# Moving three of the six modulation vectors from beside the inverse to beside the chunk scan

## The chip, the cores and the metric

The kernel runs on one core of a Trainium2 chip, as one launch. The metric is the time on the device, in microseconds (us). A core has five engines that run their own instruction streams and meet at semaphores: TensorE (PE, with its weight loads shown apart as PEld), VectorE (DVE), ScalarE (ACT), GpSimd (POOL) and SyncE (SP, which here only starts transfers). The profile is one execution, recorded by the hardware.

## The reference, cut to what matters

Two transformer blocks are computed for one sequence of 512 tokens and 1024 features. The change lies in the first one:

```python
c_act = jax.nn.silu(c)
mod = c_act @ w_ada[l] + b_ada[l]                  # [1, 6 * 1024]
shift1, scale1, gate1, shift2, scale2, gate2 = jnp.split(mod, 6, axis=-1)
h = modulate(rms_norm(x, norm_mix[l]), shift1, scale1)
proj = h @ w_in[l]
...
gdn_out = gated_deltanet(...)                      # (I + M)^-1 per chunk, then a scan over 8 chunks
swa_out = sliding_window_attention(...)
mixed = jnp.concatenate([gdn_out, swa_out], axis=-1) @ w_out[l]
x = x + gate1[:, None, :] * mixed
h2 = modulate(rms_norm(x, norm_ffn[l]), shift2, scale2)
x = x + gate2[:, None, :] * hierarchical_moe(h2, ...)
```

So `shift1`, `scale1` are needed at the start, `gate1` in the output projection, `shift2` and `scale2` for the router after it, and `gate2` at the end of the experts. The weights `w_ada` are 24 MB in float32, 4 MB for each vector. The second block (two feed-forward layers, an attention and a recurrence) follows and is not touched.

## The kernel before, in words

Activations lie transposed, 128 features on the partitions and 512 tokens along them. Float32 products are made exact by splitting each operand into a head and a rest (`wsplit`, L252, on ACT and DVE) and multiplying three times (`mm3`, L262: lines 268, 269 and 270).

**The vectors.** `ada` (L375) is a generator. Its items are pairs (g, h): half h (512 columns) of vector g. An item takes five steps. Each of the first four (L381 to L391) loads two k-tiles of the weights, 512 KB, into one of three `wraw` buffers (L384, issued by SP), and multiplies them as the moving operand by a column of silu(c): four products of 256 columns, in four strips of 32 columns of the array, which the trace shows as eight L388 instructions. They add up in a PSUM tile of the `sm` set, which has three buffers. The fifth step (L392 to L399) adds the bias (L393), copies the sums out of PSUM on ACT (L395), folds them with four small products (L397) and copies the result into `mod` (L398).

**The order of the work.** Generators are woven by hand. `weave(main, (gen, rate))` (L193) advances a filler by `rate` steps after each step of the main generator. The tile framework's planner then orders the instructions by this program order and by its own model of when they are ready; an engine runs its list strictly in that order.

The stages around the change:

- *Inverse stage* (L842 to L848). Main: `kprep` (16 steps), `mpreps` (12) and `inverse` (56), 84 steps in all. Fillers: `dense` (the projections of q, of the window attention, of v and z, 0.6 steps), `ada` for gate1, shift2, scale2 and gate2 (eight items, 40 steps, rate 0.6) and `side` (the inner products of the chunks and the window attention, 1.2). At 0.6 the 40 steps of `ada` end after 67 of the 84 main steps.
- *Scan stage* (L965 to L967). Main: `uw` (12 steps; L855) and `scan` over the eight chunks (24 steps; L887). Filler at 0.8: `swasplit` (4 steps), `bias_tables` (2), `yd_zero` (1, which zeroes 4 MB in DRAM by a POOL transfer) and `wout_swa` (L957, 16 steps: the half of the output projection whose input is the window attention). These 23 steps end after 29 of the 36 main steps.
- *Second half of the output projection* (L989 to L997): eight rounds of twelve matmuls with the router's logits between them. Before it, L971 reads scale2 and L977 shift2.

After that come the experts (`moe`), which read gate2 last. `wraw` is shared by all of this: the loads of the projections' weights (L249) and those of `ada` (L384) take the same three buffers, in the order in which SP has them.

Of the kernel before, what the change touches and what calls it, by code (L numbers as in the profile page):

```python
# [18 lines left out]
P = 128  # L19
# [11 lines left out]
# --------------------------------------------------------------------------  # L31
# host side: layout of the inputs and constants that depend on shapes alone
# --------------------------------------------------------------------------
def _mt(w, cols=None):
    """[K, M] -> [M/128, 128 (k), K/128, 128 (m)]"""
    if cols is not None:
        w = w[:, cols]
    k, m = w.shape
    return np.ascontiguousarray(w.reshape(k // P, P, m // P, P).transpose(2, 1, 0, 3))


def _cols(v):
    """[n*128] -> [128, n]"""
    return np.ascontiguousarray(np.asarray(v).reshape(-1, P).T)


def layout(a):
    o = {}
# [38 lines left out]
    # block 2  # L87
# [23 lines left out]
    def lru(n):  # L111
        w = a[n][0].reshape(4, 2, P, 2, P)  # head, k tile, k, m tile, m
        return w.transpose(2, 0, 3, 1, 4).reshape(P, 8 * 2 * P)
# [15 lines left out]
def constants():  # L129
# [8 lines left out]
    # [t, c]: t <= c / t > c inside a chunk  # L138
# [31 lines left out]
    # relative position: one-hot bucket rows and a mask row, over u  # L170
# [14 lines left out]
# --------------------------------------------------------------------------  # L185
# device side
# --------------------------------------------------------------------------
# [5 lines left out]
def weave(main, *fill):  # L193
    """the steps of main, and after each one `rate` steps of every filler (gen, rate)"""
    due = [0.0] * len(fill)
    for _ in main:
        for i, (gen, rate) in enumerate(fill):
            due[i] += rate
            while due[i] >= 1.0:
                due[i] -= 1.0  # L200
                next(gen, None)


class Net:
# [16 lines left out]
    def bt(self, shape, dt=F32):  # L221
        """a 2 KB per partition tile out of the shared set"""
# [23 lines left out]
    # ---- weights: raw f32 -> 12-bit head (f32r) + exact rest (f32r)  # L246
# [15 lines left out]
    def mm3(self, ps, wh, wl, xh, xl, kts, start=True, stop=True):  # L262
        """ps += W^T x over the k-tiles; wh/wl [128, nk*128]; xh/xl lists of [128, N]"""
# [8 lines left out]
    def mm3y(self, ps, wh, wl, xh, xl, kts, start=True, stop=True, n=3):  # L272
        """mm3 in steps of n k-tiles"""
# [10 lines left out]
    # ---- rsqrt of a small tile (x > 0), Newton on the vector engine  # L284
# [11 lines left out]
    # ---- softplus of a small tile  # L296
# [20 lines left out]
    # ---- 1/rms over the features of a T-layout activation, broadcast to all partitions  # L317
    def sumsq(self, acc, k, src):
        """acc += src^2"""
# [7 lines left out]
    def sumsq2(self, acc, k, src, hs):  # L327
        """acc[:, hs] += src[:, hs]^2, without the tensor engine or the vector engine"""
# [7 lines left out]
    def rstd_half(self, hf, *accs):  # L336
        """[P, 2]: 1/rms of the tokens of a half; the sums over the features on the tensor engine"""
# [36 lines left out]
    # ---------------------------------------------------------------- block 1  # L374
    def ada(self, items, raws=None):  # L375
        """mod[:, g] = w_ada^T silu(c) + b_ada by halves: the k-tiles as moving operand in four column tiles"""
# [49 lines left out]
    def block1(self):  # L426
# [39 lines left out]
        # statistics of x  # L466
# [5 lines left out]
        # scale1, shift1 by halves; k-tiles 0..3 of the projections of k follow the first halves  # L472
# [50 lines left out]
        # conv + silu (twice the value)  # L523
# [14 lines left out]
        def stats2(src, pst, base):  # L538
            """pst[:, i, base:base+2] = per token sums of squares over the two 64-halves"""
# [10 lines left out]
        # ---- gates  # L550
        def gates():
            # four k-tiles beside each other in the columns of the array
# [23 lines left out]
        def decays():  # L576
# [4 lines left out]
            # sum over a chunk, per head on the partitions of its half  # L581
# [12 lines left out]
        # ---- k: token major, normalised, and back  # L594
# [32 lines left out]
        # ---- decay and -M, its transpose  # L627
# [30 lines left out]
        # ---- q, v  # L658
# [11 lines left out]
        # ---- attention inside chunks, transposed, over k  # L670
# [19 lines left out]
        # ---- projections of the window attention  # L690
# [46 lines left out]
        # ---- sliding window attention  # L737
# [59 lines left out]
        # ---- z  # L797
# [7 lines left out]
        # ---- (I + M)^-1 by doubling of the diagonal blocks  # L805
# [37 lines left out]
        ada = mark("ada", self.ada([(g, h) for g in (2, 3, 4, 5) for h in range(2)]))  # L843
# [8 lines left out]
        # ---- scaled v and k, token major, behind the inverse  # L852
        vb, kd, nw = MT, kt, [None] * 4

        def uw():  # L855
# [11 lines left out]
            for i in range(4):  # L867
# [3 lines left out]
                # -w^T [d (head parity), pair, chunk parity * 64]  # L871
# [11 lines left out]
        # ---- scan over the chunks; o = s o', s = rq / 8: s rsqrt(s^2 mean(o'^2) + eps)  # L883
# [62 lines left out]
        # results of the experts: rows for the first and the second expert of a token  # L946
# [7 lines left out]
        # ---- output projection: the rows of the window attention, then those of the delta rule  # L954
# [10 lines left out]
        fill = chain(swasplit(), self.bias_tables(), yd_zero(), wout_swa())  # L965
        weave(chain(uw(), scan()), (fill, 0.8))
        drain(fill)  # L967

        # router: logits = (x * rstd * gain + shift) W = rstd * (x (gain W)) + shift W
# [34 lines left out]
    # ------------------------------------------------- block 1: mixture of experts  # L1004
    def moe(self):
# [5 lines left out]
        # the pairs of one group at a distance: its experts tend to be in demand together  # L1011
        order = [4 * g + i for i in range(4) for g in range(4)]
        NP = NE // 2
        # the results of the last pairs go to x by the tensor engine, the others by DRAM
        NL = 2

        def load(n, part=(0, 1)):
            """weights of pair n: gate | up in two halves per expert, down"""
# [15 lines left out]
        # slots beyond the last token keep finite values  # L1034
# [4 lines left out]
        # ---- normalized tokens, token-major, and a copy in DRAM  # L1039
# [13 lines left out]
        # ---- routing  # L1053
# [3 lines left out]
        def first_max(l, n, tag):  # L1057
            """the maximum, one-hot of its first place"""
# [24 lines left out]
        # [tok, tile, expert]  # L1083
# [10 lines left out]
        # tokens of the same expert before a token: in its tile, and in the tiles before (last: all)  # L1094
# [7 lines left out]
        # place of a token at its experts, from 1  # L1102
# [9 lines left out]
        # weights of the two experts  # L1112
# [20 lines left out]
        # pair: token, weights at its two experts, rows of the results  # L1133
# [6 lines left out]
        # tiles of the passes beyond the first  # L1140
        q1, q2, q3, q4 = (self.t(self.tp, [P, S], "cy" if q < 2 else "th") for q in range(4))
        # (no reuse of an index that a transfer may still read)
# [3 lines left out]
        def oindex(p, r):  # L1146
            """place of a slot's row in yd, or its token (the last pairs); its token"""
# [14 lines left out]
        def select(p, r):  # L1162
            """slots 64r..64r+63 of the two experts of the p-th pair: one-hot by token; token and weight of a slot"""
# [19 lines left out]
        def gather(p, r):  # L1183
            """their tokens, one on a partition"""
# [8 lines left out]
        def feed(xTs, hf, pt):  # L1193
            """gain and shift of the tokens, features on the partitions"""
# [19 lines left out]
        def pick(oh):  # L1214
            """the same by the tensor engine, without the way through DRAM"""
# [11 lines left out]
        def piece(p, c, o, r):  # L1227
            """512 columns of the weights of an expert of pair p"""
# [30 lines left out]
        def expert2(p, hT, idx, wv, r=0):  # L1259
            """weighted results, to DRAM; of the last pairs: in two parts, with the one-hot of the tokens by slot"""  # L1260
# [23 lines left out]
        def combine(ys, hs):  # L1284
            """x += gate * the results of the slots, at their tokens"""
# [13 lines left out]
        def ahead(p):  # L1299
            """the passes of pair p beyond the first: tokens fetched early"""  # L1300
# [11 lines left out]
        def more(p):  # L1312
            """the second and third pass of pair p"""
# [9 lines left out]
        def rest(p, r=3):  # L1323
            """the passes beyond, with weights loaded again"""
# [564 lines left out]
```

## Time and profile before

| | us |
|---|---|
| time, median of 3 runs (2240.81 to 2242.68) | 2241.49 |
| span of the profiled execution, first to last instruction | 2238.9 |
| what lies around the span, against the median | 2.6 |
| PE busy in matmuls | 2095.0 (94%) |
| PEld busy in weight loads | 1567.7 (70%) |
| DVE busy | 1078.0 (48%) |
| ACT busy | 718.2 (32%) |
| POOL busy | 202.9 (9%) |

Shares are of the span. A stretch A:B counts us from the span's start. "Idle before, releaser" in a row is the time in which the engine stood before that group and what ended it. A matmul's time in the trace includes its way through the array, so consecutive ones overlap; what one costs is read from the starts. Each float32 matmul with a float32 weight stands as two instructions.

### The profile page before, as it was taken

The page shows a single profiled execution, that of the slowest core. Times are in us where ns is not written, and L with a number is a line of the kernel's source. Part 1 is how long each engine was busy: PE and PEld are TensorE (multiplying, and loading weights), DVE is VectorE, ACT ScalarE, POOL GpSimd, SP SyncE. Part 2 cuts the span into 40 slices and gives each one's busy share as a digit, 9 for nine tenths or more (in the row PEclk, how much of TensorE's full clock was granted, in tenths as well). Part 3 has the DMA queues.
Part 4 walks back from the last instruction along what each step waited for, and adds up shares of the span by engine and source line. Part 5 has one row for each costly group of instructions (what it writes and reads, how often), then busy time and mean ns, then how long its engine had stood idle before and what let it go on. Part 6 is the DMA issues. An engine that isn't in the chain of part 4 may idle for free.

```text
span 2238.9 us, 32214 instructions
## 1 busy us (share of the span) xinstructions
PE 2095.0 (94%) x12908; PEld 1567.7 (70%) x12908; DVE 1078.0 (48%) x2071; ACT 718.2 (32%) x1197; POOL 202.9 (9%) x223
## 2 busy tenths in 40 slices
PE   5999999788888978999999899999999999999996
PEld 3677677553333427888888787878878888888886
DVE  4663655542221227553354864746564447542444
ACT  3432442122222224322222443525452243222221
POOL 3020002011111122000001300000000031000002
PEclk9999999788999988999999999999999999999998
DMA  7343315075968962323332232323222322233321
GB/s 262 112 133 105 105 48 160 29 284 215 399 238 329 382 249 95 99 90 91 102 92 82 88 83 76 113 67 113 62 99 90 108 76 81 93 89 95 98 90 38
DMA packets 93877, 294.53 MB, mean 132 GB/s; under 512 B 15746, under 2 KB 27010, under 8 KB 81404
## 3 DMA queue, kind: packets, MB, share of 16 engines
q1 hardware_dynamic: 86364, 278.03, 36.4%
q0 software_dynamic: 7328, 14.01, 1.9%
q8 instruction: 119, 1.95, 0.4%
q14 instruction: 66, 0.54, 0.1%
HBM read 286.12 MB, written 20.23 MB: 137 GB/s over the span
## 4 chain that ended last, share of the span: by engine, by line
PE 57%; DVE 3%; POOL 1%; ACT 1%; issue 1%; POOLq 0%; ACTq 0%; DVEq 0%
PE mm L269 18%; PE mm L270 18%; PE mm L268 18%; PE sm L1605 1%; DVE xl L1507 1%; PE mm L1633 1%; POOL x L1459 1%; POOL ss L334 1%; DVE cy L1458 0%; PE mm L1630 0%; ACT wh L255 0%; PE sm L1620 0%; PE sm L1757 0%; PE mm L1289 0%; PE sm L1603 0%
## 5 line engine op out<-in xcount | busy, mean ns | idle before, releaser
L268 PE MATMUL mm<-xh,wh 128*128 128x512 f32 (+1 forms) x1584 | 621.4, 395 | 8.4 <-ACT xh L1506 4.1
L269 PE MATMUL mm<-xl,wh 128*128 128x512 f32 (+1 forms) x1584 | 612.4, 387 | 4.0 <-DVE xl L1507 4.0
L270 PE MATMUL mm<-xh,wl 128*128 128x512 f32 (+1 forms) x1584 | 609.7, 386 | 0.1
L255 ACT ACTIVATE wh<-wraw 128x1024 fp32r<-128x1024 f32 (+3 forms) x282 | 274.1, 974 | 771.8 <-PE mm L269 681.4
L256 DVE TENSOR_TENSOR wl<-wraw,wh 128x1024 fp32r<-128x1024 f32 (+3 forms) x282 | 315.0, 1118 | 196.6 <-ACT wh L255 191.3
L268 PEld LDWEIGHTS mm<-xh,wh 128*128 128x128 f32 x1584 | 301.4, 191 | 81.5 <-issue 8.3
L269 PEld LDWEIGHTS mm<-xl,wh 128*128 128x128 f32 x1584 | 303.1, 191 | 66.1 <-DVE xl L1507 5.7
L270 PEld LDWEIGHTS mm<-xh,wl 128*128 128x128 f32 x1584 | 302.6, 191 | 62.9 <-issue 1.2
L334 POOL TENSOR_TENSOR ss<-ss,sq 128x256 f32<-128x256 f32 (+1 forms) x69 | 66.9, 970 | 951.6 <-ACT sq L333 935.5
L268 PE MATMUL mm<-hh,wh 128*128 128x512 f32 (+1 forms) x416 | 149.8, 360 | 0.0
L270 PE MATMUL mm<-hh,wl 128*128 128x512 f32 (+1 forms) x416 | 149.6, 360 | 0.0
L269 PE MATMUL mm<-hl,wh 128*128 128x512 f32 (+1 forms) x416 | 149.4, 359 | 0.0
L1241 PE MATMUL mm<-wmoe,xgT 128*64 128x512 f32 x512 | 128.5, 659 | 8.1 <-issue 8.1
L1241 PEld LDWEIGHTS mm<-wmoe,xgT 128*64 128x64 f32 x512 | 42.8, 152 | 83.8 <-issue 76.4
L268 PEld LDWEIGHTS mm<-hh,wh 128*128 128x128 f32 x416 | 78.1, 188 | 13.3
L269 PEld LDWEIGHTS mm<-hl,wh 128*128 128x128 f32 x416 | 78.1, 188 | 13.3
L270 PEld LDWEIGHTS mm<-hh,wl 128*128 128x128 f32 x416 | 78.0, 188 | 13.2
L1567 DVE TENSOR_TENSOR sq<-mm,rsb 128x512 f32<-128x512 f32 x44 | 30.4, 691 | 110.7 <-PE mm L270 110.7
L1562 DVE TENSOR_TENSOR cy<-mm,rsb 128x512 f32<-128x512 f32 x44 | 30.4, 691 | 91.6 <-PE mm L270 89.6
L1247 DVE SCALAR_TENSOR_TENSOR mth<-mth,mm 128x256 f32<-128x256 f32 x16 | 6.7, 420 | 114.3 <-ACT mth L1246 114.3
L1275 PE MATMUL mm<-wmoe,hT 128*64 128x512 f32 x256 | 57.9, 592 | 0.0
L1198 ACT ACTIVATE xgT<-mm,mod,gs 128x128 f32<-128x128 f32 x64 | 27.9, 462 | 77.4 <-DVE xgT L1200 69.8
(495 smaller groups left out, 2613.7 us busy)
## 6 DMA issues: line engine op xcount, KB each, us to landing
wmoe<-in_wmoe SPq DMA_DIRECT2D x96, 1024.0 KB
wraw<-in_win SPq DMA_DIRECT2D x90, 512.0 KB
wraw<-in_wgu SPq DMA_DIRECT2D x88, 512.0 KB
wraw<-in_wada SPq DMA_DIRECT2D x32, 512.0 KB
wraw<-in_wd SPq DMA_DIRECT2D x32, 448.0 KB
big<-in_wada SPq DMA_DIRECT2D x16, 512.0 KB
wraw<-in_wd SPq DMA_DIRECT2D x16, 512.0 KB
wraw<-in_wout SPq DMA_DIRECT2D x16, 256.0 KB
```

The lines of the kernel that those rows point to most:

```text
L255: self.nc.scalar.activation(h[:, :n], raw[:, :n], AF.Copy)
L256: self.nc.vector.tensor_sub(l[:, :n], raw[:, :n], h[:, :n])
L268: mm(ps, w1, xh[k], start=start and i == 0, stop=False)
L269: mm(ps, w1, xl[k], start=False, stop=False)
L270: mm(ps, w2, xh[k], start=False, stop=stop and i == nk - 1)
L334: self.nc.gpsimd.tensor_add(acc[:, hs], acc[:, hs], sq[:, hs])
L1198: s.activation(xTs[hf][:, k, :], pt[:, k, :], AF.Identity, scale=self.gs2[:, kk:kk + 1], bias=mod[:, 3, kk:kk + 1])
L1241: mm(pg_[cs, :], xT[k // 4][:, k % 4, cs], piece(p, c, k // 4 * 2048 + k % 4 * S, r), start=k == 0, stop=k == KT - 1)
L1275: mm(py[cs, :], hT[:, k, cs], piece(p, c, 4096 + k * 1024 + n * S, r), start=k == 0, stop=k == 1)
L1459: (self.nc.gpsimd if k % 2 else self.nc.vector).tensor_add(self.x[k][:, hs], self.x[k][:, hs], t[:, hs])
L1562: v.tensor_mul(t1, pp[0], rb)
L1567: v.tensor_mul(t2, pp[1], rb)
```

## The change

The list of `ada` beside the inverse is cut from eight items to two (gate1 alone). The other six, shift2, scale2 and gate2, go beside the scan: a new helper, `alternate`, takes one step of the old filler and one of `ada` in turn until both are at an end, and the filler's rate goes from 0.8 to 1.5. (Comments are taken out elsewhere in the file, which shifts line numbers.)

```diff
+def alternate(*gens):
+    gens = list(gens)
+    while gens:
+        for gen in list(gens):
+            try:
+                next(gen)
+            except StopIteration:
+                gens.remove(gen)
+                continue
+            yield
...
-        ada = mark("ada", self.ada([(g, h) for g in (2, 3, 4, 5) for h in range(2)]))
+        ada = self.ada([(2, h) for h in range(2)])
         side = chain(after(["q", "m"], inner()), after(["swaproj"], swa()))
         weave(chain(kprep(), mark("m", mpreps()), inverse()), (dense, 0.6), (ada, 0.6), (side, 1.2))
...
-        fill = chain(swasplit(), self.bias_tables(), yd_zero(), wout_swa())
-        weave(chain(uw(), scan()), (fill, 0.8))
+        ada = self.ada([(g, h) for g in (3, 4, 5) for h in range(2)])
+        fill = alternate(chain(swasplit(), self.bias_tables(), yd_zero(), wout_swa()), ada)
+        weave(chain(uw(), scan()), (fill, 1.5))
         drain(fill)
```

No buffer, tile or shape changes. Nothing waits for the name `ada` that `mark` set.

## Rows read from the trace of the kernel before

**Rows 1.** The page, TensorE's granted clock in 40 slices of 56 us.

```profile
PEclk9999999788999988999999999999999999999998
```

**Rows 2.** Stretches: us, busy us (instructions) by engine, granted clock, DMA share, GB/s.

```profile
125.00:285.00 160.00, 159.95 (x2336) 119.43 (x2334) 87.81 (x180) 52.42 (x113) 10.27 (x8) 1.00 0.36 113
285.00:349.00 64.00, 62.15 (x746) 46.10 (x746) 31.92 (x73) 25.27 (x64) 1.89 (x2) 1.00 0.29 102
349.00:369.00 20.00, 17.23 (x311) 12.85 (x309) 9.20 (x15) 9.03 (x21) 6.22 (x11) 1.00 0.42 110
369.00:404.00 35.00, 34.21 (x386) 24.95 (x386) 26.69 (x73) 6.05 (x10) 6.18 (x10) 1.00 0.34 84
404.00:433.50 29.50, 17.66 (x213) 15.03 (x211) 19.10 (x55) 3.78 (x6) 1.23 (x2) 0.68 0.06 19
433.50:466.00 32.50, 32.50 (x126) 20.56 (x125) 10.29 (x16) 8.21 (x13) 0.62 (x1) 0.92 0.61 240
...
421.00:433.50 12.50, 6.84 (x64) 6.68 (x62) 7.30 (x22) 1.26 (x2) 0.00 (x0) 0.50 0.00 0
```

**Rows 3.** Groups of instructions by line, 125 to 286 us, those of `ada`.

```profile
L388 PE MATMUL sm<-wraw,ca 128*32 128x256 f32 x184 | 16.5, 391 | 0.0
L397 PE MATMUL sm<-c_sel,sq 128*128 128x1 f32 x48 | 6.2, 250 | 0.0
...
L395 ACT COPY sq<-sm 128x512 f32<-128x512 f32 x6 | 3.5, 587 | 13.2 <-PE sm L388 13.2
...
L393 PE MATMUL sm<-c_bada,c_ident 128*128 128x4 f32 x12 | 1.7, 210 | 0.0
```

**Rows 4.** PE's timeline around one step of `ada`: start, us, what.

```profile
257.46 0.39 PE L269 MATMUL mm<-xl,wh 128*128 128x512 f32 x1
257.68 0.40 PE L270 MATMUL mm<-xh,wl 128*128 128x512 f32 x1
258.01 0.64 PE L388 MATMUL sm<-wraw,ca 128*32 128x256 f32 x8
258.58 1.15 PE L1408 MATMUL mm<-big,big 64*64 64x64 f32 x32
```

**Rows 5.** PE's timeline around the closing step of an item.

```profile
284.62 0.28 PE L393 MATMUL sm<-c_bada,c_ident 128*128 128x4 f32 x2
284.75 1.03 PE L397 MATMUL sm<-c_sel,sq 128*128 128x1 f32 x8
285.71 0.50 PE L1408 MATMUL mm<-big,big 64*64 64x64 f32 x9
```

**Rows 6.** PE's waits from 285 to 349 us: us in total, times, longest.

```profile
PE mm L1408 <- ACT xx L812: 1.2, 1, 1.2
PE sm L793 <- ACT ptS L791: 0.4, 1, 0.4
```

**Rows 7.** PE's timeline at the end of the scan.

```profile
429.44 1.08 PE L939 MATMUL sm<-c_ident,eo 128*128 128x128 f32 x4 [5.66 <-DVE eo L934]
...
434.17 0.63 PE L269 MATMUL mm<-xl,wh 128*128 128x512 f32 x1
434.59 0.63 PE L270 MATMUL mm<-xh,wl 128*128 128x512 f32 x1
...
438.43 0.39 PE L270 MATMUL mm<-xh,wl 128*128 128x512 f32 x1
```

**Rows 8.** SP's timeline: the issue of one load of `ada`.

```profile
100.09 0.37 SPq L384 DMA_DIRECT2D wraw<-in_wada  x1
```

**Rows 9.** Stretches of 1 us after that issue; the last number is GB/s.

```profile
101.00:102.00 1.00, 1.00 (x7) 0.35 (x5) 1.00 (x3) 0.24 (x1) 0.96 (x1) 0.50 0.79 121
102.00:103.00 1.00, 1.00 (x10) 0.19 (x9) 0.90 (x5) 0.39 (x1) 0.00 (x0) 0.50 0.90 350
103.00:104.00 1.00, 1.00 (x7) 0.85 (x4) 0.90 (x5) 0.63 (x1) 0.02 (x1) 0.55 0.22 70
```

**Rows 10.** SP's waits from 300 to 450 us: us in total, times, longest.

```profile
SPq L249 <- DVE wl L256: 104.3, 12, 26.2
```

## The prediction

> **What bounds the kernel now.** I read the page first, for the share of each engine and the clock in 40 slices. TensorE is the busiest engine, and its clock stands below full speed longest in the slices from 392 to 560 us [rows 1]; the first of them holds most of the scan. Next I read busy times by stretch, with borders where the stages of the code begin and end [rows 2]. Three things are to be seen there.
>
> In the part of the inverse stage that holds `ada`, 125 to 285 us, matmuls cover 159.95 of 160 us. After the last `ada` step, 285 to 349 us, they still cover 62.15 of 64. So TensorE sets the pace there, with or without `ada`, and work that is taken out shortens the stage.
>
> In the scan stage, 349 to 433.5 us, PE is idle for 2.77 us in the first stretch (`uw`), 0.79 in the second (the scan while the old filler lasts) and 11.84 in the third (the filler has run out after 29 of 36 main steps): 15.40 us. In the last of them PE waits for VectorE, once for 5.66 us [rows 7]: the scan's own chain sets the end there, and TensorE has room.
>
> At 404 to 433.5 us the granted clock is 0.68 of full speed on average, and from 421 on 0.50, the lower of its two levels, 1.2 GHz, after stretches in which PE had little to do. The second half of the output projection starts at that level: its matmuls follow each other in 0.42 us [rows 7], where in the inverse stage it is 0.22 [rows 4].
>
> **What the change removes.** 24 load-and-multiply steps and six closing steps leave the inverse stage. In 125 to 286 us there are 184 L388 instructions, eight to a step, so 23 of the 24 lie there, and six closings: 48 L397, 12 L393 [rows 3]. What one costs PE I read from starts, since ends overlap: a step from 258.01 to 258.58, 0.57 us [rows 4]; a closing from 284.62 to 285.71, 1.09 us [rows 5]. That is 24 x 0.57 + 6 x 1.09 = 13.7 + 6.5 = 20.2 us.
>
> Not all of it need come off, because `ada` is independent work that also covers waits. The stretch behind it shows what PE loses without such cover: 1.85 us in 64, two waits for ScalarE of 1.2 and 0.4 us for the most part [rows 2, 6]. On the 140 us that remain of the first stretch this would be 4.0 us. With `ada` it was 0.05. I take 2.0, the middle, as the two waits are single events at the end of a stage, where the fillers run dry. The stage gets **18.2 us shorter** (16.2 to 20.2).
>
> The Trainium skill speaks against this term: Perfetto Trace Analysis, Identifying the Most-Contended Engine, says that matmul occupancy is no measure of TensorE's headroom and that the busy share of weight loads is one. By it TensorE had a quarter of the stretch free, and the term would be nothing. The trace does not bear it out so far: the share of weight loads is 75% with `ada` and 72% without [rows 2], so it doesn't rise when the work thins out, and no wait shows up in which that quarter could lie.
>
> **What it adds to the scan stage.** The same 20.2 us of PE work. At 1.5 steps per main step, in turn, 36 main steps advance 54 filler steps: all 23 old ones and 30 of `ada` are 53. So the filler now lasts to the very end, and the old one is spread out as well (0.75 for 0.8).
>
> Of the 15.40 us of idle PE the last wait of 5.66 us, where PE stands until VectorE has normalised the last pair of chunks [rows 7], is one main step long and can take 1.5 steps of the filler, some 1.5 us; 4.2 remain. Usable are 11.2 us, and the stage **grows by 9.0 us**. Bounds: 4.8, if all idle time is used; 12.5, if half of it is.
>
> Entering and leaving another shape of matmul costs PE 0.1 us: 0.33 us from L270 to L388, 0.22 between two of the same shape [rows 4]. I take nothing more, since the 0.57 was read between two such changes and in the scan a step mostly stands at one as well; if each stood alone, 24 x 0.1 = 2.4 us is the other end.
>
> **The clock.** PE's busy 6.84 us from 421 to 433.5 ran at half speed, and so did ten matmuls from 434.17 to 438.43, 0.2 us dearer each [rows 2, 7]. With matmuls in the idle stretch before it, the clock may stay up: 0 to 2.0 + 3.4 = 5.4 us back. I take **3.0**, as 4.2 us of idle remain in front.
>
> **What else moves.** SP issues 24 loads of 512 KB, 0.37 us each [rows 8], 8.9 us in a stage of some 90, past eight x loads and the loads of `wout`; nothing in the scan waits for SP otherwise. A load's bytes are in 3.1 us after its issue (121 + 350 + 70 KB in the 1 us stretches that follow) [rows 8, 9]. With three `wraw` buffers and about one `ada` step in 3.5 us this is covered; the DMA share in the scan stage is 0.42, 0.34 and 0.06 [rows 2], and 12.6 MB more are 36 us at the 350 GB/s of [rows 9], beside what POOL's queue sends in the stage (the 4 MB of `yd_zero` and the bias tables). If that cover is gone, see the second rival. On POOL nothing is added. ScalarE gets six copies of 0.59 us [rows 3] and six small ones, some 4 us, where it is busy for 18.9 of 84.5 [rows 2]. VectorE gets nothing. An `sm` buffer is held by `ada` for most of the stage, one of three, and the scan takes two for its outputs; I put this at 0, as those outputs are off the chain of states, and the bound upwards is inside the 12.5 above. L971 and L977 need items that end at two thirds of the filler, well ahead of them; gate2, the last, is needed in the experts.
>
> **The sum.** -18.2 + 9.0 - 3.0 = -12.2 us. The profiled span is 2238.9, so 2226.7; with the 2.6 us around it, **2229.3 us** against the median of 2241.5. This case reaches from -20.2 + 4.8 - 5.4 = -20.8 (2220.7) to -16.2 + 12.5 + 2.4 = -1.3 (2240.2).
>
> **Rivals.**
>
> *No room in the scan.* PE's gaps there are mostly too short or sit where no filler is ready, and the 20.2 us come on top: -18.2 + 20.2 = +2.0, **2243.5**. For it: while the old filler lasts, only 0.79 us in 35 are idle [rows 2], so two thirds of the added steps meet a full engine. Against: that filler is spread too and reaches into the empty third stretch.
>
> *Late loads, slower.* Place: SP's list and the three `wraw` buffers in the scan stage. A `wout` load waits for its buffer until VectorE has split an earlier one; SP stood so for 104.3 us, once for 26.2 [rows 10]. An `ada` load behind it in the list starts late, and PE, in order, stands with the scan's own matmuls queued behind L388. Price: if the three buffers act as one, each `ada` load takes 3.1 + 0.57 = 3.7 us, 24 of them 88 us; the eight `wout` loads, half the bytes, 18 us (2.3 each, between 1.6 and 3.1); six closings 6.5: 113 for the stage's 84.5. -18.2 + 28.5 = +10.3, **2251.8**. It decides once PE's waits before L388 pass 12 us in all, where the gain is gone, and makes the kernel slower by over 0.2% from 17. Against: those 104 us kept nobody waiting, as the loads came early, and there are three buffers.
>
> *The inverse is a chain.* By the rule above, PE's covered time hides slack, the inverse's own chain sets the end, and nothing comes off: +9.0 - 3.0 = +6.0, **2247.5**. Against: 2.9% idle after `ada` has ended.
>
> *It doesn't move.* The planner may take the steps forward again, into the inverse stage; then the time stays at **2241.5**. Three buffers allow a few steps of this, not 24.
>
> **Chances.** 0.2% of the time, 4.5 us, is about what can be told from no change: faster is under 2237.0, slower over 2246.0. The forecast has 0.72 (0.68 of it under 2237.0), everything hidden and more, under 2220, 0.06, no room 0.08, doesn't move 0.04, late loads 0.06, the chain 0.04. Faster 0.74, same 0.16, slower 0.10. The range is 2220 to 2244: the forecast's own and the two cases without a difference; left out are 0.06 below and 0.10 above.
>
> **What would show it.** Right: only 64 L388 instructions on `wraw` ahead of the scan stage, those of gate1; the scan stage begins some 18 us earlier with PE still over 97% covered in the inverse; it lasts about 94 us instead of 84.5; idle PE from the old filler's end to L939 falls by more than half, and the clock there rises above 0.68. The forecast is wrong if PE waits for `in_wada` before L388 for more than a few us, if waits of PE in the inverse stage pass 4 us, or if the scan's last L939 comes later against the start of `uw` by more than 15 us.

## The result, and the profile after

The change makes the kernel slower: 2257.15 us median (2242.94 to 2258.79, six runs) against 2242.09 for the kernel before measured beside it, a ratio of 1.0062 with a 95% interval of [1.0041, 1.0082]. (One of the six runs of the kernel before, 2394.84 us, was slow and is left out of the ratio.) Forecast were 2229.3 us and a range up to 2244. A second set of twelve runs gave 2254.49 and 1.0056 [1.0041, 1.0072].

Line numbers are 13 higher than before up to the end of the scan: `ada` loads at L397, multiplies at L401, adds the bias at L406, copies on ACT at L408, folds at L410; the split of weights is L268 on ACT and L269 on DVE. The scan's transposes (L939 before) are L952.

The page of the kernel after, with its granted clock in 40 slices:

```profile
span 2255.4 us, 32203 instructions
PE 2108.8 (93%) x12908; PEld 1577.7 (70%) x12908; DVE 1081.2 (48%) x2071; ACT 717.6 (32%) x1197; POOL 202.7 (9%) x223
PEclk9999999788899998999999999999999999999998
```

The span is 16.5 us longer with the same number of matmuls. Stretches of the kernel after (us, busy us and instructions of PE, PEld, DVE, ACT and POOL, granted clock, DMA share, GB/s), the first two being the inverse stage and the next two `uw` and the scan with its filler:

```profile
125.00:273.00 148.00, 144.66 (x2131) 111.97 (x2124) 88.95 (x180) 48.03 (x103) 10.39 (x9) 0.99 0.12 37
273.00:337.80 64.80, 63.25 (x751) 46.65 (x749) 33.69 (x77) 26.64 (x66) 1.89 (x2) 1.00 0.31 109
337.80:367.80 30.00, 24.86 (x370) 16.13 (x362) 9.62 (x13) 8.31 (x19) 9.96 (x16) 0.87 0.85 238
367.80:425.90 58.10, 57.00 (x580) 39.00 (x578) 32.36 (x86) 8.74 (x17) 3.98 (x6) 0.86 0.41 125
425.90:448.00 22.10, 14.91 (x174) 10.04 (x174) 12.31 (x41) 3.52 (x7) 0.00 (x0) 0.70 0.47 145
...
337.80:447.90 110.10, 96.77 (x1118) 65.16 (x1110) 54.19 (x140) 20.58 (x43) 13.95 (x22) 0.83 0.54 160
```

The same span of work, from VectorE's first operation of `uw` to the start of the last normalisation of the scan (the last row above), in the kernel before:

```profile
351.10:428.60 77.50, 62.94 (x876) 47.09 (x872) 50.97 (x137) 16.17 (x31) 13.63 (x22) 0.91 0.28 73
```

Three readings. The scan stage starts at 337.8 instead of 351.1 us, so the inverse gave back 13.3 us. The stage then takes 110.1 us instead of 77.5. And of PE's idle time there, 14.6 us before, 13.3 are left: the moved work did not fill it. PE is busy for 33.8 us more, far beyond the 20.2 that were moved, since the granted clock fell from 0.91 to 0.83 and matmuls at the lower of the two levels follow each other in 0.43 us (below) for 0.22 [rows 4]. Up to the first result of the second half of the output projection (459.8 for 438.9) the loss is 21 us; 4.5 come back later. Those 4.5 can't be put down to the change: a second profile of the same kernel (run 10) takes 1803.0 us from there to its end, this one 1795.6 and the kernel before 1800.1.

TensorE hardly waits for the moved loads. Waits in the kernel after from 338 to 460 us (us in total, times, longest), PE's first, then ScalarE's and SP's:

```profile
PE sm L952 <- DVE eo L947: 7.4, 2, 6.1
PE mm L890 <- DVE mn L882: 3.6, 1, 3.6
PE sm L401 <- DMA wraw<-in_wada: 1.6, 1, 1.6
...
ACT wh L268 <- DMA wraw<-in_wout: 17.8, 5, 5.9
ACT sq L408 <- PE sm L401: 9.0, 3, 5.0
...
SPq L397 <- PE sm L401: 43.7, 13, 7.8
SPq L262 <- PE sm L401: 14.8, 7, 4.9
```

SP stands until an L401 has freed a buffer, 43.7 us before moved loads and 14.8 before loads of `wout`. ScalarE waits 17.8 us for `wout`, where before no wait of ScalarE for a transfer stood in this stretch. How such a wait reaches TensorE shows in the timeline of the kernel after:

```profile
357.90 0.98 PE L890 MATMUL mm<-big,mn 64*64 64x64 f32 x32
...
360.45 0.63 ACT L268 ACTIVATE wh<-wraw 128x512 fp32r<-128x512 f32 x1 [3.64 <-DMA wraw<-in_wout]
...
361.11 2.28 DVE L269 TENSOR_TENSOR wl<-wraw,wh 128x512 fp32r<-128x512 f32 x1 [3.99 <-ACT wh L268]
363.31 0.68 DVE L882 TENSOR_TENSOR mn<-big,kbf 128x512 f32<-128x512 f32 x1
...
364.14 1.61 PE L890 MATMUL mm<-big,mn 64*64 64x64 f32 x32 [3.58 <-DVE mn L882]
```

The late load holds ACT, ACT holds DVE's L269, and behind that stands L882, which makes an operand of `uw`. PE waits 3.58 us, and its next 32 instructions take 1.61 us for 0.98: the clock has fallen meanwhile. This is the one place where the whole chain is seen; PE's other waits here are shorter. The wait at the scan's end ([rows 7]) is still there, 6.06 us for 5.66, and the second half of the projection still starts at the lower clock:

```profile
448.73 1.09 PE L952 MATMUL sm<-c_ident,eo 128*128 128x128 f32 x4 [6.06 <-DVE eo L947]
...
455.58 0.63 PE L282 MATMUL mm<-xl,wh 128*128 128x512 f32 x1
456.01 0.63 PE L283 MATMUL mm<-xh,wl 128*128 128x512 f32 x1
```

### The profile page after: what moved, and what is told of

Same layout as the page of the kernel before. It is cut to its first block, busy times and chain, and to the rows that moved or that the text cites. A ratio compares the mean times of both kernels' runs of the same rounds, so it can differ in the third digit from the quotient of the medians.

```text
span 2255.4 us, 32203 instructions
## 1 busy us (share of the span) xinstructions
PE 2108.8 (93%) x12908; PEld 1577.7 (70%) x12908; DVE 1081.2 (48%) x2071; ACT 717.6 (32%) x1197; POOL 202.7 (9%) x223
## 5 line engine op out<-in xcount | busy, mean ns | idle before, releaser
L268 ACT ACTIVATE wh<-wraw 128x1024 fp32r<-128x1024 f32 (+3 forms) x282 | 274.0, 974 | 780.1 <-PE mm L282 681.2
L269 DVE TENSOR_TENSOR wl<-wraw,wh 128x1024 fp32r<-128x1024 f32 (+3 forms) x282 | 318.5, 1130 | 202.0 <-ACT wh L268 194.9
L281 PEld LDWEIGHTS mm<-xh,wh 128*128 128x128 f32 x1584 | 301.3, 191 | 83.1 <-issue 10.2
L281 PEld LDWEIGHTS mm<-hh,wh 128*128 128x128 f32 x416 | 78.1, 188 | 13.4
L282 PEld LDWEIGHTS mm<-hl,wh 128*128 128x128 f32 x416 | 78.1, 188 | 13.3
```

What stands on the lines that cost most here:

```text
L268: self.nc.scalar.activation(h[:, :n], raw[:, :n], AF.Copy)
L269: self.nc.vector.tensor_sub(l[:, :n], raw[:, :n], h[:, :n])
L281: mm(ps, w1, xh[k], start=start and i == 0, stop=False)
L282: mm(ps, w1, xl[k], start=False, stop=False)
```

## The experiments

In the table, *start* is VectorE's first operation of `uw` in us (PE's first lies 0.8 us earlier), *stage* runs from there to the first result of the second half of the output projection, *low* is the time in it at the lower clock; these come from one profile each. The ratio is to the kernel before measured beside it. A single profile has its own spread: the ten kernels that have the same work ahead of `uw` as the kernel after start at 335.9 to 340.6 (338.4 on average), the three that have the work of the kernel before at 351.1 to 354.1 (353.0). The inverse gave back 13.3 us in the pair of profiles above and 14.6 between these averages.

| run | median us | ratio | start | stage | low |
|---|---|---|---|---|---|
| before | 2239 to 2242 | 1 | 351.1 | 87.7 | 23.9 |
| after | 2257.15 | 1.0062 [1.0041, 1.0082] | 337.8 | 122.0 | 47.8 |
| 1 items left out | | | 338.6 | 87.7 | 20.5 |
| 2 no loads | | | 339.3 | 102.0 | 17.1 |
| 3 own buffers | 2245.64 | 1.0032 [1.0014, 1.005] | 336.2 | 103.8 | 17.1 |
| 4 other PSUM set | 2251.34 | 1.006 [1.0042, 1.0078] | 339.0 | 112.9 | 34.1 |
| 5 both | 2244.64 | 1.0017 [1.0003, 1.003] | 335.9 | 104.5 | 23.9 |
| 6 gate2 behind, rest thinner | 2246.63 | 1.0028 [1.0017, 1.0039] | 352.3 | 89.8 | 23.9 |
| 7 all behind | 2259.76 | 1.0086 [1.0071, 1.0102] | 340.4 | 121.7 | 54.6 |
| 8 before, spread | 2242.98 | 1.0008 [0.9995, 1.0021] | 354.1 | 85.4 | 17.1 |
| 9 all behind, own buffers | 2256.89 | 1.0066 [1.0052, 1.008] | 337.8 | 125.5 | 44.4 |
| 10 after again | 2254.49 | 1.0056 [1.0041, 1.0072] | 340.6 | 118.5 | 37.5 |
| 11 gate2 behind | 2236.40 | 0.9979 [0.9966, 0.9992] | 346.2 | 89.4 | 20.5 |
| 12 a third, in turn | 2239.21 | 0.9994 [0.9978, 1.001] | 347.6 | 91.1 | 17.1 |
| 13 two thirds, in turn | 2245.90 | 1.0025 [1.0012, 1.0038] | 343.4 | 101.1 | 20.5 |
| 14 after, ready work added | 2258.42 | 1.008 [1.0065, 1.0094] | 338.4 | 118.4 | 10.2 |
| 15 before, the same added | 2252.16 | 1.0051 [1.0036, 1.0065] | 353.7 | 94.6 | 10.2 |

### 1 and 2: without the items, without their loads

```diff
-        ada = self.ada([(g, h) for g in (3, 4, 5) for h in range(2)])
+        v.tensor_copy(mod[:, 3:6, :], mod[:, 0:3, :])
...
-        weave(chain(uw(), scan()), (fill, 1.5))
+        weave(chain(uw(), scan()), (fill, 0.8))
```

> Leaves out the six moved items (shift2, scale2 and gate2 are copies of other vectors), so it gives the price of the moved work in each place. Theories: (L) the moved loads share three raw buffers and SP's list with the wout loads, and their lateness stretches the scan stage; (C) the added PE work and the clock that falls in the scan stage stretch it, whatever the loads do; (S) the sm buffers in PSUM do. All three expect the inverse stage as short as in the changed kernel (uw begins near 338 us) and the scan stage as in the kernel before (about 88 us from the first step of uw to the first result of the second half): about 2229 us, 13 below the kernel before.

In the second run the items stay, but multiply a fixed table instead of loading:

```diff
-                raw = raws[n % len(raws)] if raws else self.t(self.wp, [P, 1024], "wraw")
+                raw = fixed
...
-                nc.sync.dma_start(raw..., self.A["wada"]...)
```

> The six moved items multiply a table that lies in the SBUF for good, without their 24 loads (so their values are not the reference's); their PE, ScalarE and PSUM work stays. (L) expects the scan stage to fall from 122 us to 100 or less, about 2236 us or less. (C) and (S) expect 115 us or more, 2250 us or more.

Other values of the vectors change the router's choice of experts: with 12392 and 12578 matmul instructions for 12908 these runs took 2166.96 and 2166.23 us, so only the stage is compared here. Without the items the stage is 87.7 us, as before, and begins at 338.6: what the items cost is 12.5 to 13.3 us beside the inverse and 34.3 beside the scan. Without their loads they cost 14.3. So the loads stand for 20 us of the profiled loss (theory L had asked for a little more, a stage of 100 us or less), and 14.3 of work are on top, not the 9.0 of the forecast. The stretch up to the last normalisation without the loads:

```profile
339.30:429.40 90.10, 83.18 (x1118) 57.50 (x1110) 52.94 (x139) 20.57 (x42) 13.60 (x22) 0.96 0.24 63
```

Against the kernel before PE has 20.2 us more of busy time, as much as was moved (at a clock of 0.96 for 0.91), and 7.6 less of idle (6.9 for 14.6). Against the kernel after it lacks 20.0 us: 6.4 of idle, and 13.6 of busy time with the same number of instructions (1118), at a clock of 0.96 for 0.83. Two thirds of what the loads cost here are thus PE's own work at the lower clock.

### 3, 4 and 5: buffers of their own, another PSUM set

```diff
+                raw = pairs[n % 3]      # (sqT[0], sqT[1]), (sqT[2], sqT[3]), (skT, vtok)
...
+                for q in range(2):
+                    nc.sync.dma_start(raw[q], self.A["wada"][g, :, k + q, h * S:(h + 1) * S])
```

> The moved loads go into three pairs of tiles that the window attention has left (sqT, skT, vtok), not into wraw, so the wout loads have wraw to themselves; SP's list stays shared. (L) expects more than half of the growth of the scan stage to go, 105 us or less and 2240 us or less. (C) and (S) expect 117 us or more, within 4 us of the changed kernel's 2257.

```diff
-            ps = self.pst([P, S], "sm")
+            ps = self.pst([P, S], "mm")
...
-            po = self.pst([P, 4], "sm")
+            po = self.pst([P, 4], "mm")
```

> The moved items take their PSUM tiles from the mm set (five) in place of the sm set (three), so that the scan has sm to itself. (S) expects the time to fall by over 6 us, to 2251 or less. (L) and (C) expect it within 4 us of the changed kernel's 2257.

> Both remedies at once: the moved vectors load into buffers of their own and take their PSUM from the mm set, all else as after. If the two waits (theories L and S) are separate and add up, the scan stage is shorter than with own buffers alone (103.8 us): 94 to 97, near the 94 that was forecast, and the time 2235 to 2239 us. If the PSUM tile only hurt because the late loads held it long, nothing is gained on top of the own buffers: 102 to 105 and 2243 to 2247. Theory C (the work itself and the clock): the same as with own buffers alone, with low clock of about 17 us left.

Own buffers take back 18.2 us of the profiled stage, and no ScalarE wait for `wout` is left. In time they take back less: the ratio falls from 1.0062 and 1.0056 to 1.0032, some 5 to 7 us or about half of the loss, and the intervals still touch (the profiled run, 2242.14 us, is one of the fastest of its five). Theory L had the stage right and the time, 2240 or less, wrong. With both remedies (run 5) the ratio is 1.0017, clear of both, some 9 to 10 us. The same 12.6 MB come in the same stage, in 48 transfers for 24, so it is not the bytes. The stretch up to the last normalisation:

```profile
336.20:428.00 91.80, 85.37 (x1118) 57.27 (x1110) 51.32 (x138) 20.56 (x42) 13.52 (x22) 0.96 0.59 182
```

Against the kernel after, 11.4 us of PE's busy time are gone with the same number of instructions (clock 0.96 for 0.83), and 6.9 of idle. Against the kernel before, 22.4 us of busy time were added and 8.1 of idle used. PSUM settled little: the fourth run's profile is 9 us better than after's, its ratio is not, and both remedies together give the stage of the third alone (104.5 for 103.8), with a ratio whose interval overlaps the third's.

### 7 and 9: behind the old filler instead of in turn

```diff
-        fill = alternate(chain(swasplit(), self.bias_tables(), yd_zero(), wout_swa()), ada)
+        fill = chain(swasplit(), self.bias_tables(), yd_zero(), wout_swa(), ada)
```

> All six items beside the scan at the same rate of 1.5 and in the shared wraw buffers, but behind the old filler instead of in turn with it. Theory L in its form that the loads of wout stand behind loads that wait for a buffer: no load of wout of the first half stands behind one of the moved loads, so ScalarE waits less than 3 us for in_wout, the scan stage is 100 to 106 us and the time 2242 to 2247. L in the form that 24 loads through three buffers take their time wherever they stand, or theory S (PSUM): 113 to 122 and 2251 to 2258.

> All six items behind the old filler as in the run before (stage 121.7 us, 54.6 of it at the lower clock), but loaded into three buffers of their own as in the run with own buffers (103.8 us, 17.1). Theory L (the shared buffers are the cost, in either order): the stage is 102 to 107 us and the time 2240 to 2246. Theory T (thin work: where the steps of the moved vectors are TensorE's only filler, they leave it so much waiting that the clock falls, whoever owns the buffers): the stage stays at 115 to 122 us with over 40 us at the lower clock, and the time at 2250 to 2260.

Run 7 refutes the theory in the form I had given it: no load of `wout` of the first half stands behind a moved one, ScalarE waits 1.4 us for them where it waited 17.8, and the stage is as long as ever. Run 9 has the buffers of run 3 and a stage like run 7's, with 44.4 us at the lower clock and 2256.89 us, as theory T had it (its stage of 115 to 122 us came out at 125.5), so who owns the buffers doesn't decide here. What differs between runs 3 and 9 is the order alone, and their ratios' intervals don't touch. In run 9 the old filler's last product starts at 378.12 us, and the moved steps are PE's only filler from there. Its timeline:

```profile
381.89 0.62 PE L405 MATMUL sm<-sqT,ca 128*32 128x256 f32 x4 [0.35 <-DMA sqT<-in_wada]
...
384.21 0.67 PE L924 MATMUL mm<-cosT,big 64*64 64x64 f32 x14 [0.42 <-DVE cosT L918]
385.47 0.68 PE L915 MATMUL mm<-S,big 64*64 64x64 f32 x16 [0.58 <-DVE S L927]
386.66 0.33 PE L924 MATMUL mm<-cosT,big 64*64 64x64 f32 x2 [0.51 <-DVE cosT L918]
387.32 1.10 PE L924 MATMUL mm<-cosT,big 64*64 64x64 f32 x14 [0.33 <-DVE cosT L918]
```

and its stretches:

```profile
380.00:387.40 7.40, 5.20 (x82) 2.97 (x80) 5.19 (x20) 1.22 (x2) 0.00 (x0) 1.00 0.93 313
387.40:401.00 13.60, 13.33 (x132) 9.43 (x132) 4.87 (x12) 0.69 (x2) 1.37 (x2) 0.50 0.40 129
...
337.80:451.10 113.30, 97.97 (x1118) 65.30 (x1114) 52.64 (x139) 20.57 (x42) 15.04 (x22) 0.85 0.48 147
```

After several short waits for the scan's own chain the clock falls at 387.4, and from there PE is busy 13.33 us of 13.60 at half speed. The same fourteen L924 take 1.10 us for 0.67. Only one of the waits shown is for a moved load (0.35 us). A run in this order without the loads was not made, so whether the loads or the thin steps themselves leave PE these gaps is not shown.

### 10: the same kernel again

> The changed kernel once more, nothing edited, for the spread of its runs against the clock that each was granted. If the clock makes most of the loss, the runs at a mean clock of 0.966 or more take under 2247 us and those at 0.964 or less over 2252, with nothing else different between them. If the late loads cost what they cost by the order of the instructions alone, the runs lie within 3 us of 2257 at any clock.

Twelve runs go from 2240.87 us at a mean clock of 0.970 to 2263.86 at 0.959. Neither expectation has it whole: the times follow the clock, but the run at 0.966 took 2251.3. A straight line through these and the six first runs falls by 1.73 us for each 0.001 of clock and stands at 2249.9 at 0.966; the runs of the kernel before measured beside them stand at 2242.6 there. So at that clock about 7 us of the loss are left, and the rest goes with the clock, whose mean is 0.963 for 0.9675. But this is the mean over the whole kernel, and it does not say where the clock was low. The profiled run, at 0.959 the slowest of the twelve, has *less* low clock in the stage than the kernel after at 0.963 (37.5 us for 47.8) and ends it at the same time (459.1 for 459.8 us); it loses its 6.7 us behind the stage, where 125 us are at the lower clock for 104. What the low clock of the stage costs can't be read from this run.

### 14 and 15: ready work added

```diff
+        def warm():
+            while True:
+                pw = self.pst([P, S], "mm")
+                for i in range(4):
+                    mm(pw[:, :P], ident, ident, start=i == 0, stop=i == 3)
+                yield
...
-        weave(chain(uw(), scan()), (fill, 1.5))
+        weave(chain(uw(), scan()), (fill, 1.5), (warm(), 0.5))
```

> The changed kernel with 18 further filler steps in the scan stage, each of four 128x128 products that nothing reads and that wait for no load (about 0.6 us each, 11 us in all). If TensorE's waiting there is what lowers the clock (theory T), time at the lower clock in the stage falls from 37 to 48 us to under 25, and the stage grows by less than 6 us or shrinks, though 11 us of work were added. If the clock falls for another reason, or costs little, the stage grows by 9 to 14 us: 128 to 136, and 2264 to 2270 us.

> The same 18 steps in the kernel before, as the price to compare with. If the scan before has room (15.4 us of idle TensorE, as the forecast had it) and the lower clock at its end goes, the stage is 84 to 92 us (87.7 without) and the time within 3 us of the kernel before. If added work comes on top there too, 96 to 100 us and 2249 to 2253.

The estimate in these expectations is wrong. A step stands as eight instructions and takes PE 1.0 us, as the starts in run 15 show, so the 18 steps are 18 us of work and not 11:

```profile
371.96 1.05 PE L969 MATMUL mm<-c_ident 128*128 128x128 f32 x8
372.94 0.98 PE L877 MATMUL mm<-big,mn 64*64 64x64 f32 x32
```

Run 14, stretch up to the last normalisation, and below it the kernel after in the profile of run 10:

```profile
338.40:444.80 106.40, 99.94 (x1262) 73.49 (x1254) 52.58 (x139) 20.99 (x44) 13.95 (x22) 1.00 0.56 167
...
340.60:447.20 106.60, 93.05 (x1118) 62.09 (x1110) 52.52 (x140) 20.91 (x44) 13.92 (x22) 0.87 0.55 165
```

Run 15:

```profile
353.70:439.20 85.50, 75.60 (x1018) 61.92 (x1014) 52.81 (x137) 16.46 (x31) 13.61 (x22) 0.98 0.25 66
```

With 18 us of work added to the kernel after, the clock of the stretch is 1.00 instead of 0.83, and the stretch is no longer than without: 106.4 us against 110.1, and against 106.6 at a clock of 0.87 in the profile of run 10. PE's idle time there falls from 13.3 and 13.6 us to 6.5, and the time at the lower clock in the stage to 10.2. The stage and its clock are as the first expectation of run 14 had it. In time the addition costs before 12.7 us (2252.16 for 2239.42), and after 4.0 to 5.4 (ratios 1.0080 against 1.0062 and 1.0056; their intervals overlap). The difference, some 7 to 9 us, is an estimate of what keeping the clock up gives back, on the assumption that the added work costs the same in both kernels otherwise; it is about half of the loss. It leaves out that the kernel before gains by the clock too (low clock 10.2 us for 23.9). So the low clock follows from how thinly the stage is filled: ready work in the gaps takes it away. That runs 3 and 9 differ through the order alone is shown; by which waits the order does it, and why the granted clock of one and the same program differs from run to run, is not.

Run 15 also tests the forecast's own ground: 18 us of ready work, spread over the stage of the kernel *before*, use 4.7 us of its idle time (9.9 are left of 14.6), where the forecast had called 11.2 usable. The stage gets 6.9 us longer, with less of it at the lower clock, and the kernel 12.7 us slower. The time is that of the second expectation, the stage of 94.6 us lies between the two.

### 6, 8, 11, 12 and 13: how much, and where

```diff
-        ada = self.ada([(2, h) for h in range(2)])
+        ada = self.ada([(g, h) for g in (2, 3, 4) for h in range(2)])
...
-        ada = self.ada([(g, h) for g in (3, 4, 5) for h in range(2)])
-        fill = alternate(chain(swasplit(), self.bias_tables(), yd_zero(), wout_swa()), ada)
-        weave(chain(uw(), scan()), (fill, 1.5))
+        ada = self.ada([(5, h) for h in range(2)], tag="mm")
+        fill = chain(swasplit(), self.bias_tables(), yd_zero(), wout_swa(), ada)
+        weave(chain(uw(), scan()), (fill, 0.95))
```

Run 6 has this with the rate of `ada` beside the inverse at 0.45, run 11 at 0.6.

> Only gate2 (10 of the 30 moved steps) goes to the scan, behind the old filler and not in turn with it, in the shared wraw buffers and with PSUM from the mm set; shift2 and scale2 stay beside the inverse. If the cost comes from loads that stand ahead of the loads of wout, this order has hardly any: the inverse gets some 4.4 us shorter (a third of 13.3), the scan stage 0 to 3 us longer than 87.7, the time 2236 to 2241 us. If each moved step costs in the scan what it cost in the change (34.3 us for 30 steps, 11.4 for ten), the stage is 99 us and the time 2248 to 2250.

> The run with gate2 alone beside the scan, with the four items that stay beside the inverse at the rate of 0.6 (as in the kernel before) instead of 0.45. If the inverse had given nothing back there because its steps were spread thinner, it now ends 4 us earlier: the first product of the scan stage at 345 to 348 us, the stage at 88 to 91 and the time 2236 to 2240 us, below the kernel before. If a third of the steps is simply not worth anything there, the start is at 350 to 353 and the time 2243 to 2247, as in that run.

Run 8 is the kernel before with its filler at 0.64 for 0.8; it fits the second expectation in time and the first in the stage. The shorter stage is no gain: it starts 3.0 us later and ends at 439.5 us for 438.8.

> The kernel before with nothing moved, its old filler spread over the whole scan (rate 0.64 for 0.8). If the filler's reach into the scan's empty end is worth something by itself (the forecast's usable idle time and its clock term), the scan stage is 2 to 5 us shorter than 87.7 and the low clock in it well under 23.9 us. If the scan's own chain sets the time at any filling, it is 87 to 90 us and the kernel's time the same as before.

Runs 12 and 13 are the kernel after with fewer items beside the scan: (5,) at a rate of 0.95 and (4, 5) at 1.23.

> A third of the change as it was made: gate2 alone goes beside the scan, in turn with the old filler, in the shared wraw buffers and with its PSUM from the sm set; shift2 and scale2 stay beside the inverse at 0.6. If what counts is how much is moved (thirty steps pass what the scan can cover, ten do not), the start of the scan stage is at 345 to 348 us, the stage at 88 to 92 and the time 2235 to 2241, as when gate2 stood behind the filler with the other PSUM set. If the order in turn or the PSUM set is what costs, the stage is 96 to 102 (up to a third of 34.3 on top of 87.7) and the time 2244 to 2250.

> Two thirds of the change: scale2 and gate2 in turn with the old filler (rate 1.23, 43 steps over 35), shift2 stays beside the inverse. If the scan has room for some ten steps and each one more comes on top, with its share of lower clock, this lies between the third (2239.2, stage 91.1) and the whole (2255, stage 122): start of the stage near 342, stage 98 to 108, 2244 to 2250 us. If the cost has a threshold near the whole amount, it is as cheap as the third: stage 92 to 96, and 2234 to 2240 us.

In turn, the price of ten steps rises: one third, two thirds and all of them bring the start forward by 3.5, 7.8 and 13.3 us and lengthen the stage by 3.4, 13.4 and 34.3 (30.8 in the second profile of the whole). Only the first third is paid for, as the first expectations of runs 12 and 13 had it. The amount and the loads aren't told apart here, as ScalarE's waits for `wout` rise too: 2.4, 18.6 and 17.8 us. Run 11 is faster than both kernels, by 0.21% against before (0.9979 [0.9966, 0.9992]): the start comes 4.9 us earlier and the stage is 1.7 longer. Its ten steps stand from 397.83 us on, behind the old filler, where the kernel before has its emptiest stretch (404 us on, [rows 2]); up to the last normalisation:

```profile
346.20:424.70 78.50, 69.92 (x959) 51.66 (x954) 51.99 (x138) 17.62 (x35) 13.57 (x22) 0.93 0.45 125
```

One microsecond longer than before (77.5), with 7.0 us more of busy PE and 6.0 less of idle. Run 6 has the same scan stage and no gain, because its inverse ended at 352.3, which its expectation did not foresee. With the same items at 0.45, PE is idle for 5.1 us from 100 us to that start, for 2.2 in run 11; that is 2.8 of the 6.1 us, and the rest is not explained.

## Why the prediction was wrong, point by point

**The inverse, -18.2.** Right in kind, too large by some 4 to 5 us: the start came forward by 13.3 (14.6 between averages). PE's idle time there rose to 4.9 us (two stretches above: 3.34 and 1.55) from 1.9 [rows 2], 3.0 where 2.0 were forecast. Some of the rest is clock: 6.8 us around 121 and 138 us ran at the lower level, which can hold up to 3.4 us of work and was taken as unchanged. By the Trainium skill's rule against this term (Perfetto Trace Analysis, Identifying the Most-Contended Engine), as the prediction read it, nothing would have come off; 13.3 us did, and the share of weight loads (112 of 148 us) is no sign of a quarter to spare here.

**The scan, +9.0: the first step that failed.** "Usable are 11.2 us" took the idle time of the whole stage as room for a filler that is spread over the whole stage. Without loads 7.6 us were used (run 2), with loads in their own buffers 8.1 (run 3), with ready work 4.7 (run 15). Most of the idle time sits at the end, after the old filler has run out (11.84 of 15.40 us), and ten steps put there fit (run 11). Where the old filler lasts only 0.79 us in 35 were idle, as the rival *No room* said. The same work lengthened the stage by 14.3 us (run 2) and 16.1 (run 3), above the 12.5 that I had called the bound and below that rival's 20.2. By itself this makes the change worth nothing: -13.3 and +14 to 16.

**The clock, -3.0.** Wrong in sign. It was argued that more matmuls in the stage keep the clock up. Without loads, or with loads in their own buffers, they do a little: 17.1 us at the lower clock for 23.9 (runs 2 and 3). As the change was made there are 47.8 us, and 54.6 and 44.4 in runs 7 and 9, where the moved steps alone fill the end of the scan. The Trainium skill (TensorE: Matmul & The Clock Gate, A second HAM failure mode: psum-queue depth-cycling) tells of a kernel whose TensorE stands still briefly and often between groups of matmuls and whose clock goes up and down with it. The traces agree in this pattern, though the waits here are others: in the kernel after the stage has six stretches at the lower clock, in the one before one.

**Queues and loads, 0: the step that failed most.** "With three `wraw` buffers ... this is covered" put at nothing what measured 20.0 us of the stage by leaving out the loads (run 2) and 18.2 by giving them buffers (run 3). It did not fail as the rival *Late loads* had it. That rival named the place (SP's list and the three buffers) and the side, and came within 5.4 us of the time. But its test was PE's wait before L388, over 12 us in all, and that is 3.4 us in the whole kernel; since its path was not the one taken, the closeness of its time is luck. The wait went to ScalarE (17.8 us) and from there to VectorE and PE (3.58 us where it is shown), and most of the price was paid at the lower clock. By the profiles of the kernels before and after and of run 2 the sum is -13.3 for the inverse, +14.3 for the work, +20.0 for the loads with the clock, -4.5 behind the stage: +16.5 where -12.2 were forecast. The forecast costed ScalarE by its busy time and did not ask what stands behind a split that waits for a transfer.

**The signs.** The text held the forecast wrong if the scan's last transposes come over 15 us later against the start of `uw`: 110.9 us for 78.3. PE's waits in the inverse were to stay under 4 us; its idle time there is 4.9. The third sign, PE's wait for `in_wada`, did not show (1.6 us in the stage).

**What stays open.** The causes overlap: late loads make waits, and waits lower the clock. Run 3 removes about half of the loss by buffers and run 5 some two thirds, run 14 brings the clock up by ready work, run 9 shows that buffers alone don't do it in another order. A share of about half of the loss in time for the clock is the estimate from runs 14 and 15; these runs don't come nearer.

## What to carry to other kernels

Idle time is room only for work that can be put where the idle time is: count it by stretch, and give a filler no more steps than the stretch with room can take. A load that is moved must be followed through every in-order engine that waits for its neighbours in the buffer set, not only through its consumer. And a filler need not hold TensorE's clock up: where the moved steps alone filled the end of the scan it was low for 44 to 55 us, so a stage can lose more than the work that was put into it.

## What was not expected of the hardware

The same program took between 2240.87 and 2263.86 us, and its time followed the mean granted clock (0.970 and 0.959 at these two ends), 1.73 us for each 0.001. Adding 18 us of matmuls that nobody reads left a stretch of 106.6 to 110.1 us at 106.4: it ran at the higher clock throughout (1.00 for 0.83 and 0.87) and had 7 us less of idle PE.
